# Retention two row tiles ahead of the output projection, and a later, halved split of one weight piece

## The chip, the cores and the metric

The kernel runs on one core of a Trainium2 chip. The metric is the device time of one launch in microseconds (us). Work is done by TensorE (PE), VectorE (DVE), ScalarE (ACT) and GpSimd (POOL); SyncE (SP) issues DMAs. Each engine executes its own list of instructions strictly in order, and an instruction that waits for another engine holds everything behind it on its own engine.

## The reference

Two layers are applied to 512 latent tokens and 128 context tokens of width 1024. Each layer mixes tokens in three groups of heads (A window attention, B neighbourhood attention, C retention), puts the concatenated result through one output projection, and then runs a mixture of 16 experts. The change sits between retention and the output projection:

```python
# group C, per head: chunks of 128 tokens, a state S carried from chunk to chunk, both directions
inner = einsum(einsum(qc, kc) * dmat, vc)
cross = einsum(qc, S) * xi
...
def _retention_out(o, g, gn_w):
    mu = o.mean(-1); var = square(o - mu).mean(-1)          # per token and head
    on = (o - mu) * rsqrt(var + eps) * gn_w
    return silu(g) * on

def _mixer_latent(...):
    oa, ob, oc = window_attention, neighbourhood_attention, retention
    cat = concatenate([oa, ob, _retention_out(oc, gc, gn_w)], -1)   # 512 + 256 + 256 columns
    return cat @ w_out                                              # 1024 x 1024
...
x = layernorm(alpha * x + g1 * mix)
x = layernorm(alpha * x + g2 * expert_choice(x))                    # 16 experts, w_gate_up and w_down
```

## The kernel before

**Tiles.** The 640 tokens are five row tiles of 128: t = 0 to 3 latent, t = 4 context. For each tile `cs` holds the concatenated mixer output, transposed and split into a rounded high half and a remainder. `split` makes the two: ACT writes the high half (L344), DVE or POOL subtracts it for the low half (L345). One product of the output projection is three matmuls, high x high, high x low, low x high (L348, L349, L350 in `mm3`). Columns 0 to 767 of `cs` come from the attentions, columns 768 to 1023 from retention, so the products ko = 6 and 7 of a tile need its retention.

**Output weights.** They come as four pieces of 1 MB, which `weights` loads and splits: pieces 1 and 2 (the upper and lower rows of the first 512 output columns), 3 and 4 (those of the second 512). The names in the rows below are `wh_...` and `wl_...` for the two halves, `w_...` for the raw piece. Piece 1 is split by DVE, piece 2 by POOL (`WO`), piece 3 by DVE, piece 4 by POOL.

**Retention of a tile.** `retention(t, cs)` forms q.k (PE, L1221), multiplies by the decay into the work piece `AT` (DVE, L1225), scales q (DVE, L1230), forms the output `po` (PE, L1239 and L1243), and normalises it: mean (L1247, L1248), subtraction into the work piece `dd` (L1252), square on ACT (L1253), variance (L1255, L1256, L391), inverse root on POOL (L392), and two multiplications (L1259, L1260). Then PE transposes `dd` (L691, two matmuls) and the result is split into `cs`. `AT` and `dd` of all tiles come from one pool named "wr" with two pieces, which alternate, so each `dd` has the same piece as the `dd` of the tile before: L1252 of a tile must wait until L691 of the tile before has read it.

**Order.** NR tiles of retention are made while attention B still runs (`projection`). Then comes a loop over the five tiles: for tile t the first output half is computed (24 matmuls), mixed by `run_all` with the retention of a later tile and with the transposes of z and the router product of tile t - 1 (L1387, ACT L1391, L1395). A second loop computes the second output half of each tile with pieces 3 and 4. `gated` (L1373 to L1375 on DVE) joins an output half to the residual z. A scheduler lays the instructions of each engine into their final order, so the order in the code is only where it starts from; `tc.issue_after(ins)` adds one edge, and only for instructions on the engine of `ins`.

**Slots.** Big tiles share 25 slots of 1 MB, handed out in turn as they come free. `Ahead.fill` issues the loads of the next weights into them, from output weights to expert weights (wgu, wdn).

Of the kernel before, what the change touches and what calls it, by code (L numbers as in the profile page):

```python
# [24 lines left out]
NT = NTOK // 128  # L25
# [49 lines left out]
YS = 1  # L75
PR = "ro"
PGS = "gs"
NR = 1
WG = 1
WO = "0101"  # L80
PZ = "orz"
# [41 lines left out]
AH_P = 1  # L123
KP = 2
# [118 lines left out]
def hybrid_backbone_kernel(ctx: ExitStack, tc: tile.TileContext, a: dict):  # L243
# [41 lines left out]
    V, S, G, T = nc.vector, nc.scalar, nc.gpsimd, nc.tensor  # L285
    queue = [nc.sync]

    def ld(out, in_):
        return queue[0].dma_start(out, in_)
# [3 lines left out]
    def f32(x):  # L293
        return x.bitcast(F32)
# [14 lines left out]
    def weights(n, keep, parts=1, after=None, E=V, s_after=None):  # L309

        if n < 9:
            ahead.fill(n, keep)
            raw = ahead.next()
            hi, lo = sl.get(F32R, "wh"), sl.get(F32R, "wl")
        else:
            hi = sl.get(F32R, "wh")
            ahead.fill(n, keep)
            raw = ahead.next()
            lo = sl.again(ahead.spare, F32R, "wl") if ahead.spare is not None else sl.get(F32R, "wl")
            ahead.spare = raw  # L320
        if s_after is not None:
            for i in range(parts):
                w = 2048 // parts
                s = slice(w * i, w * i + w)
                with tc.issue_after(s_after):
                    S.activation(hi[:, s], raw[:, s], AF.Copy)
                with tc.issue_after(after):
                    E.tensor_tensor(lo[:, s], raw[:, s], f32(hi[:, s]), op=ALU.subtract)  # L328
        elif after is not None:
            with tc.issue_after(after):  # L330
                split(hi, lo, raw, parts, E)
        else:
            split(hi, lo, raw, parts, E)
        if n < 9:
            sl.free(raw)
        return hi, lo
# [3 lines left out]
    def split(hi, lo, src, parts=1, E=V):  # L340
        w = src.shape[-1] // parts
        for i in range(parts):
            s = (Ellipsis, slice(w * i, w * i + w)) if parts > 1 else (Ellipsis,)
            hi_op[:] = [S.activation(hi[s], src[s], AF.Copy)]  # L344
            lo_op[:] = [E.tensor_tensor(lo[s], src[s], f32(hi[s]), op=ALU.subtract)]  # L345
# [403 lines left out]
    def mixer(l, h, A, bg):  # L749
# [401 lines left out]
        def states():  # L1151
# [52 lines left out]
            C.update(S0=S0, Sv=Sv, DT=DT, xi=xi)  # L1204
            yield

        def retention(t, cs):
            qC, vcx, gC, Sv, DT, xi = (C[k] for k in ("qk", "vcx", "g", "Sv", "DT", "xi"))
            kC, vC, cxC = qC[:, 1024:2048], vcx[:, 0:1280], vcx[:, 1280:2048]

            def qk(j, x):
                r, aa = rows(j), j // 2
                if t < 4:
                    return (qC if x == 0 else kC)[r, 512 * aa + 128 * t:512 * aa + 128 * t + 128]
                return cxC[r, 256 * x + 128 * aa:256 * x + 128 * aa + 128]
            AT = work("wr")
            ATv = AT.rearrange("p (a h i) -> p a h i", a=2, h=2)
            pas = [psB(), psB()]
            for aa in range(2):
                for hh in range(2):  # L1220
                    T.matmul(pas[hh][:, 128 * aa:128 * aa + 128], qk(2 * aa + hh, 1), qk(2 * aa + hh, 0),  # L1221
                             start=True, stop=True)
            for hh in range(2):
                pa = pas[hh]
                V.tensor_tensor(ATv[:, :, hh, :], pa[:, 0:256].rearrange("p (a i) -> p a i", a=2),  # L1225
                                DT.rearrange("p (a h) i -> p a h i", a=2)[:, :, hh, :], op=ALU.mult)
            if t < 4:
                o = 1024 + 512 * (t % 2)
                qx = m0[0][:, o:o + 512]
                V.tensor_tensor(qx.rearrange("p (a d i) -> p a d i", a=2, d=2),  # L1230
                                qC[:, 0:1024].rearrange("p (a i) -> p a i", a=2)[:, :, None, 128 * t:128 * t + 128]
                                .to_broadcast([128, 2, 2, 128]), xi, op=ALU.mult)
            yield
            po = psA()
            for aa in range(2):
                if t < 4:
                    for d in range(2):
                        o = 256 * aa + 128 * d
                        T.matmul(po[:, 128 * aa:128 * aa + 128], qx[:, o:o + 128],  # L1239
                                 Sv[:, t, aa, d].rearrange("p h e -> p (h e)"), start=(d == 0), stop=False)  # L1240
                for hh in range(2):
                    o = 128 * aa + 64 * hh
                    T.matmul(po[:, o:o + 64], ATv[:, aa, hh, :], vC[:, 256 * t + o:256 * t + o + 64],  # L1243
                             start=(t == 4), stop=(t == 4 or hh == 1))
            p4 = po[:, 0:256].rearrange("p (h e) -> p h e", h=4)
            mu = sm.tile([128, 4], F32, name="mu", tag="mu")
            V.tensor_reduce(mu, p4, axis=AX.X, op=ALU.add)  # L1247
            V.tensor_scalar(mu, mu, 1.0 / HD, None, op0=ALU.mult)  # L1248
            dd = work("wr")
            d4 = dd[:, 0:256].rearrange("p (h e) -> p h e", h=4)  # L1250
            s4 = dd[:, 256:512].rearrange("p (h e) -> p h e", h=4)
            V.tensor_tensor(d4, p4, mu[:, :, None].to_broadcast([128, 4, 64]), op=ALU.subtract)  # L1252
            S.activation(dd[:, 256:512], dd[:, 0:256], AF.Square)  # L1253
            var = sm.tile([128, 4], F32, name="var", tag="var")
            V.tensor_reduce(var, s4, axis=AX.X, op=ALU.add)  # L1255
            V.tensor_scalar(var, var, 1.0 / HD, None, op0=ALU.mult)  # L1256
            rs = sm.tile([128, 4], F32, name="rs", tag="rs")
            rsqrt(rs, var, 4, "rsv")
            V.tensor_tensor(d4, d4, rs[:, :, None].to_broadcast([128, 4, 64]), op=ALU.mult)  # L1259
            V.tensor_mul(dd[:, 0:256], dd[:, 0:256], gC[:, 256 * t:256 * t + 256])  # L1260
            yield
            split(cs[:, 768:1024], cs[:, 1792:2048], ctx_T(dd, 2))

# [31 lines left out]
        def projection():  # L1295
# [4 lines left out]
            yield from prep()  # L1300
            for t in range(NR):
                css[t] = sl.get(F32R, "cs")
# [42 lines left out]
        zs, bss, started, o_last = [], [], set(), []  # L1345
# [141 lines left out]
        wo = [weights(AH_P, KP, E=G if WO[i] == "1" else V) for i in range(2)]  # L1487
        for t in range(NT):
            ret = iter(())
            for u in range(t + 2):  # L1490
                if u == NT or u < NR or u in started:
                    continue
                started.add(u)
                if u < 4:
                    css[u] = sl.get(F32R, "cs")
                ret = retention(u, css[u])
                if u == t:
                    drain(ret)
                else:
                    next(ret)  # L1500
            cs = css[t]
            z = hf.get(F32, "z")
            ld(z, (a["xtok"] if l == 0 else xres)[128 * t:128 * t + 128])
            if l and RZ:
                if t == 0:
                    gb = sl.get(F32, "ln2")
                    in_row_b(a["ln2g"][l - 1:l], gb[:, 0:1024])
                    in_row_b(a["ln2b"][l - 1:l], gb[:, 1024:2048])
                G.tensor_tensor(z, z, gb[:, 0:1024], op=ALU.mult)
                G.tensor_tensor(z, z, gb[:, 1024:2048], op=ALU.add)  # L1510
                if t == NT - 1:
                    sl.free(gb)
            if t < 4:
                split(cs[:, 0:512], cs[:, 1024:1536], catA[:, 512 * t:512 * t + 512])
                src = catB.rearrange("p (j n) -> p j n", j=2)[:, :, 128 * t:128 * t + 128]
                split(cs[:, 512:768].rearrange("p (j n) -> p j n", j=2),
                      cs[:, 1536:1792].rearrange("p (j n) -> p j n", j=2), src)
            if t == 3:
                sl.free(catA)
                hf.free(catB)  # L1520
            zs.append(z)
            bss.append(m1[0][:, 1664 + 12 * t:1676 + 12 * t].rearrange("p (n x) -> p n x", n=2))
            if t < 4:
                drain(run_all(PZ, o=out_half(t, 0, wo), r=ret, z=first_logits(t - 1) if t else iter(())))
            else:
                drain(ret)
# [7 lines left out]
            G.memset(early[0][:, 1024 * i + 512:1024 * i + 768], 0.0)  # L1534
        for x in early[1]:
            G.memset(x[64:96], 0.0)
        wo += [weights(AH_P, KP, E=G if WO[2 + i] == "1" else V) for i in range(2)]
        g1.append(gates(1))
        for t in range(4):
            if t == IW:  # L1540
# [654 lines left out]
```

## Time and profile before

| | before |
|---|---|
| median of 3 runs | 1911.55 us (1911.55 to 1911.81) |
| profiled execution, its own time | 1910.83 us |
| its span | 1909.1 us, so 1.7 us lie around it |
| busy | PE 95%, DVE 60%, ACT 22%, POOL 13% |
| chain that ended last | PE 56%, DMA 35%, DVE 5% |

The span is what the profile covers; the time is what a run reports. PE works in nearly all of the span, so idle time of PE in the mixing part is what other engines can add or take. The chain goes through DMA in 35% of the span, in the expert part.

### The profile page before, as it was taken

The page shows a single profiled execution, that of the slowest core. Times are in us where ns is not written, and L with a number is a line of the kernel's source. Part 1 is how long each engine was busy: PE and PEld are TensorE (multiplying, and loading weights), DVE is VectorE, ACT ScalarE, POOL GpSimd, SP SyncE. Part 2 cuts the span into 40 slices and gives each one's busy share as a digit, 9 for nine tenths or more (in the row PEclk, how much of TensorE's full clock was granted, in tenths as well). Part 3 has the DMA queues.
Part 4 walks back from the last instruction along what each step waited for, and adds up shares of the span by engine and source line. Part 5 has one row for each costly group of instructions (what it writes and reads, how often), then busy time and mean ns, then how long its engine had stood idle before and what let it go on. Part 6 is the DMA issues. An engine that isn't in the chain of part 4 may idle for free.

```text
span 1909.1 us, 34582 instructions
## 1 busy us (share of the span) xinstructions
PE 1804.8 (95%) x14223; PEld 901.1 (47%) x14223; DVE 1137.1 (60%) x2968; ACT 423.9 (22%) x898; POOL 242.0 (13%) x188
## 2 busy tenths in 40 slices
PE   6999999899999999999879999998899999999995
PEld 3866777773333332222257767787533333222222
DVE  3654537566565655475586555574685757465657
ACT  2354533221000000000153655322200000000002
POOL 3200002221100000000061000121300000000003
PEclk9999999998999999999989999998899999999998
DMA  9333544289999999999933343325999999999994
GB/s 375 117 134 138 200 152 134 108 322 347 397 398 397 397 398 400 401 408 415 400 115 131 127 141 135 107 83 209 345 399 400 399 397 399 398 398 407 408 416 165
DMA packets 95886, 554.62 MB, mean 291 GB/s; under 512 B 13818, under 2 KB 18832, under 8 KB 36336
## 3 DMA queue, kind: packets, MB, share of 16 engines
q1 hardware_dynamic: 89776, 532.71, 70.7%
q0 software_dynamic: 5952, 19.69, 4.3%
q8 instruction: 112, 1.84, 0.4%
q14 instruction: 46, 0.38, 0.1%
HBM read 526.31 MB, written 26.05 MB: 289 GB/s over the span
## 4 chain that ended last, share of the span: by engine, by line
PE 56%; DMA 35%; DVE 5%; issue 2%; ACT 1%; POOL 0%; SPq 0%; DVEq 0%; ACTq 0%; POOLq 0%
DMA w<-wgu 22%; DMA w<-wdn 10%; PE pA L1723 10%; PE pA L348 7%; PE pA L349 6%; PE pA L350 6%; PE pA L1727 5%; PE pB L1723 3%; PE pB L356 2%; PE pC L813 2%; PE pB L1727 2%; PE pA L517 2%; PE pA L917 1%; PE pB L1395 1%; PE pA L1485 1%
## 5 line engine op out<-in xcount | busy, mean ns | idle before, releaser
L1723 PE MATMUL pA<-w,xT 128*32 128x512 f32 x4096 | 488.3, 597 | 12.0 <-DMA w<-wgu 9.3
L1723 PEld LDWEIGHTS pA<-w,xT 128*32 128x32 f32 x4096 | 130.0, 110 | 326.3 <-issue 275.7
L1727 PE MATMUL pA<-w,xT 128*32 128x512 f32 x2048 | 263.8, 592 | 0.0
L1723 PE MATMUL pB<-w,g 128*32 128x512 f32 x1920 | 229.8, 596 | 7.1 <-DMA w<-wdn 7.1
L1727 PEld LDWEIGHTS pA<-w,xT 128*32 128x32 f32 x2048 | 66.2, 110 | 153.6 <-issue 153.0
L1723 PEld LDWEIGHTS pB<-w,g 128*32 128x32 f32 x1920 | 61.2, 110 | 154.9 <-issue 122.4
L1727 PE MATMUL pB<-w,g 128*32 128x512 f32 x960 | 124.8, 592 | 0.0
L1642 DVE STREAM_TRANSPOSE g<-z 32x128 f32<-32x128 f32 x384 | 116.2, 303 | 6.4
L1642 DVE STREAM_TRANSPOSE catB<-xg 32x256 f32<-32x256 f32 x240 | 104.4, 435 | 4.0
L348 PE MATMUL pA<-hhi,wh 128*128 128x512 f32 x224 | 92.0, 411 | 0.0
L350 PE MATMUL pA<-hhi,wl 128*128 128x512 f32 x224 | 88.2, 396 | 0.6 <-DVE wl L328 0.6
L349 PE MATMUL pA<-hlo,wh 128*128 128x512 f32 x224 | 88.2, 394 | 0.0
L1805 POOL DMA_INDIRECT acc<-catB,idx x22 | 31.3, 1424 | 437.6 <-DVE catB L1801 437.6
L1765 ACT ACTIVATE z<-pA 128x512 f32<-128x512 f32 x18 | 10.7, 597 | 336.8 <-DVE xT L1659 165.6
L1642 DVE STREAM_TRANSPOSE g<-xg 32x128 f32<-32x128 f32 x240 | 72.6, 303 | 3.9
L345 DVE TENSOR_TENSOR wl<-w,wh 128x1024 fp32r<-128x1024 f32 (+2 forms) x46 | 54.5, 1220 | 33.4 <-ACT wh L344 13.9
L1623 POOL DMA_INDIRECT xg<-znd,idx x30 | 35.1, 1171 | 293.4 <-DVE catB L1642 238.6
L348 PE MATMUL pA<-wh,cs 128*128 128x512 f32 x160 | 68.0, 426 | 0.5 <-DVE gC L1140 0.3
L344 ACT ACTIVATE wh<-w 128x1024 fp32r<-128x1024 f32 (+2 forms) x50 | 53.7, 1119 | 61.9 <-DMA w<-win 25.0
L1727 PEld LDWEIGHTS pB<-w,g 128*32 128x32 f32 x960 | 31.1, 110 | 72.6 <-issue 72.6
L348 PE MATMUL pA<-wh,hhi 128*128 128x256 f32 x192 | 59.5, 313 | 5.7 <-ACT hhi L344 3.8
L350 PE MATMUL pA<-wh,cs 128*128 128x512 f32 x160 | 64.5, 405 | 0.0
(530 smaller groups left out, 2918.7 us busy)
## 6 DMA issues: line engine op xcount, KB each, us to landing
w<-wgu SPq DMA_DIRECT2D x256, 1024.0 KB, 21.5
w<-wdn SPq DMA_DIRECT2D x128, 1024.0 KB, 21.3
wada<-wada SPq DMA_DIRECT2D x48, 1024.0 KB, 4.9
w<-win SPq DMA_DIRECT2D x20, 1024.0 KB, 7.1
w<-wout SPq DMA_DIRECT2D x8, 1024.0 KB, 5.2
znd<-z SPq DMA_DIRECT2D x8, 512.0 KB, 5.7
acc<-z SPq DMA_DIRECT2D x8, 512.0 KB, 14.8
bias<-bias SPq DMA_DIRECT2D x8, 384.0 KB, 4.8
```

The costliest lines, as they stand in the source:

```text
L344: hi_op[:] = [S.activation(hi[s], src[s], AF.Copy)]
L345: lo_op[:] = [E.tensor_tensor(lo[s], src[s], f32(hi[s]), op=ALU.subtract)]
L348: T.matmul(out, lh, rh, start=first, stop=False)
L349: T.matmul(out, lh, rl, start=False, stop=False)
L350: return T.matmul(out, ll, rh, start=False, stop=last).ins
L356: T.matmul(out, (lh, ll)[x], (rh, rl)[y], start=first, stop=last)
L517: T.matmul(pm[32 * g:32 * g + 32, :], mst[:, k, :], w[:, 512 * g:512 * g + 512], start=(k == 0), stop=(k == 7))
L813: T.transpose(pt[:, 128 * b:128 * b + 128], s[:, o + 128 * b:o + 128 * b + 128], ident)
L1623: r = G.indirect_dma_start(out=xg[0:CAP, 0:1024], out_offset=None, in_=znd[l], in_offset=IndirectOffsetOnAxis(ap=idx[:, e:e + 1], axis=0))
L1642: sq_last[:] = [V.transpose(out, rows.rearrange("p (k q f) -> p k q f", q=4, f=32)[:, :, q, :])]
L1723: last_of["T"] = T.matmul(p[32 * g:32 * g + 32], x[:, 64 * ko + 32 * i:64 * ko + 32 * i + 32], w[:, 512 * n:512 * n + 512], start=(ko == 0 ...
L1727: last_of["T"] = T.matmul(p[32 * g:32 * g + 32], x[:, 512 + 32 * ko:544 + 32 * ko], w, start=first, stop=last).ins
```

## The change

Three things change in both layers. `NR` goes from 1 to 2, so the retention of tile 1 is also made while attention B runs. The loop starts the retention of tile t + 2 beside the first output half of tile t, where it was t + 1. The split of piece 3 becomes two halves of 128x1024 where it was one of 128x2048, and its DVE instructions get an edge behind the last instruction (L1260, now L1262) of the last retention; ACT's part of it has no edge. Lines of the retention stand two further down in the new file.

```diff
-NR = 1
+NR = 2
...
+        r_last = []
+
         def retention(t, cs):
...
-            V.tensor_mul(dd[:, 0:256], dd[:, 0:256], gC[:, 256 * t:256 * t + 256])
+            r_last[:] = [V.tensor_mul(dd[:, 0:256], dd[:, 0:256], gC[:, 256 * t:256 * t + 256]).ins]
...
-            for u in range(t + 2):
-                if u == NT or u < NR or u in started:
+            for u in range(t + 3):
+                if u >= NT or u < NR or u in started:
                     continue
...
-        wo += [weights(AH_P, KP, E=G if WO[2 + i] == "1" else V) for i in range(2)]
+
+        wo.append(weights(AH_P, KP, 2, after=r_last[0]))
+        wo.append(weights(AH_P, KP, E=G))
```

On PE, before, the end of the first output half in layer 0: the retention of tiles 3 and 4 (L1243 reads `vcxC`, the values) and the transposes of tile 3 (L691). Here tile 4's q.k and output products (rows 4 to 9) stand ahead of tile 3's transposes.

```order
L1243 MATMUL pA<-vcxC_1865,work_86 128x64 [waits DVE_49]
L1239 MATMUL pA<-S_102_2672,m_101_2647 128x128 x2
L1243 MATMUL pA<-vcxC_1865,work_86 128x64 x2
L1221 MATMUL pB<-vcxC_1865 128x128 [waits PE_49]
L1221 MATMUL pB<-vcxC_1865 128x128
L1221 MATMUL pB<-vcxC_1865 128x128 [waits DVE_49]
L1221 MATMUL pB<-vcxC_1865 128x128
L1243 MATMUL pA<-vcxC_1865,work_86 128x64 [waits DVE_49] x2
L1243 MATMUL pA<-vcxC_1865,work_86 128x64 x2
L691 MATMUL pC<-cst,work_86 128x128 [waits DVE_49]
```

The transposes of tile 4 stood 24 rows further down, behind twelve matmuls of the second output half (`wh_3288` is piece 3); these are the last rows of those and what follows.

```order
L348 MATMUL pA<-wh_3288,cs_2909 128x512
L349 MATMUL pA<-wl_3289,cs_2909 128x512
L350 MATMUL pA<-wh_3288,cs_2909 128x512
L691 MATMUL pC<-cst,work_86 128x128 [waits DVE_49,PE_49]
L691 MATMUL pC<-cst,work_86 128x128
```

On PE now, the same place: the last output products of tile 4's retention (L1245), the rest of tile 3's first half (`cs_3071`, `wh_2995` is piece 2), the transposes of tile 4, those of z, the router product, and then the second half.

```order
L1245 MATMUL pA<-vcxC_1865,work_86 128x64 x2
L1397 MATMUL pB<-m_106_2894,work_85 128x16 x2
L349 MATMUL pA<-wl_2996,cs_3071 128x512
L350 MATMUL pA<-wh_2995,cs_3071 128x512
L348 MATMUL pA<-wh_2995,cs_3071 128x512
L349 MATMUL pA<-wl_2996,cs_3071 128x512
L350 MATMUL pA<-wh_2995,cs_3071 128x512
L691 MATMUL pC<-cst,work_86 128x128 [waits DVE_49,PE_49]
L691 MATMUL pC<-cst,work_86 128x128
L1389 MATMUL pC<-cst,z_3162 128x128 [waits DMAHW4_49]
L1389 MATMUL pC<-cst,z_3162 128x128 x3
L1397 MATMUL pB<-m_106_2894,work_85 128x16 [waits Activation_49]
```

Tile 4's transposes have moved from behind twelve matmuls of the second half to five matmuls behind the products that they depend on.

On PE now, a little earlier: the transposes of tile 1 (first two rows), the six matmuls of tile 1 that need them (`cs_2947`), and the transposes of tile 2.

```order
L691 MATMUL pC<-cst,work_86 128x128 [waits DVE_49]
L691 MATMUL pC<-cst,work_86 128x128
L348 MATMUL pA<-wh_2995,cs_2947 128x512 [waits Activation_49]
L349 MATMUL pA<-wl_2996,cs_2947 128x512
L350 MATMUL pA<-wh_2995,cs_2947 128x512 [waits DVE_49]
L348 MATMUL pA<-wh_2995,cs_2947 128x512
L349 MATMUL pA<-wl_2996,cs_2947 128x512
L350 MATMUL pA<-wh_2995,cs_2947 128x512
L691 MATMUL pC<-cst,work_86 128x128 [waits DVE_49,PE_49]
L691 MATMUL pC<-cst,work_86 128x128
L1389 MATMUL pC<-cst,z_3009 128x128 [waits DMAHW1_49,PE_49]
```

Between the transposes of tile 2 and of tile 3 there now stand four L1389, six matmuls of tile 2, four L1397 and two L1223. Before, whole output halves lay between the transposes of two tiles.

On DVE, the low half of piece 3, before (third row), ahead of the normalisation of tiles 3 and 4:

```order
L345 TENSOR_TENSOR cs_3033<-pC,cs_3033 128x256 [waits Activation_49]
L1225 TENSOR_TENSOR work_86<-pB,m_101_2647 128x2x128 [waits PE_49]
L345 TENSOR_TENSOR wl_3289<-w_3286,wh_3288 128x2048 [waits DMAHW0_49]
L1402 COPY m_106_2894<-pB 128x16 [waits PE_49]
L1373 TENSOR_TENSOR work_86<-pA,catB_1836 128x512 [waits PE_49]
L1247 TENSOR_REDUCE mu<-pA 128x4 [waits PE_49]
```

Now its two halves stand behind the last multiplication of tile 4's retention:

```order
L1262 TENSOR_TENSOR work_86<-work_86,gC_1866 128x256 [waits DVE_49]
L345 TENSOR_TENSOR wl_3289<-w_3286,wh_3288 128x1024 [waits DMAHW0_49]
L345 TENSOR_TENSOR wl_3289<-w_3286,wh_3288 128x1024
L345 TENSOR_TENSOR cs_419<-pC,cs_419 128x256 [waits Activation_49]
L1404 COPY m_106_2894<-pB 128x16 [waits PE_49]
```

Further up, on SP of layer 0, the load of piece 2 has moved from directly behind that of piece 1 to behind the four stores of `o_st` (L1193) and two loads of z. POOL's split of piece 2, which the load of piece 3 waits for (it goes into piece 2's raw slot), moves with it.

## Rows read from the trace of the kernel before

**Rows 1.** The page's chain that ended last, by engine.

```profile
PE 56%; DMA 35%; DVE 5%; issue 2%; ACT 1%; POOL 0%; SPq 0%; DVEq 0%; ACTq 0%; POOLq 0%
```

**Rows 2.** Waits of PE, 320 to 402 us: total, times, longest.

```profile
PE pC L691 <- DVE work L1260: 3.5, 1, 3.5
PE pC L1387 <- DVE z L1374: 1.6, 1, 1.6
PE pA L1243 <- DVE work L1225: 0.8, 1, 0.8
PE pB L1395 <- ACT work L1391: 0.5, 1, 0.5
```

**Rows 3.** Timeline of PE in layer 1: start, duration, instruction.

```profile
1294.49 0.69 PE L691 MATMUL pC<-cst,work 128*128 128x128 f32 x2 [3.52 <-DVE work L1260]
```

**Rows 4.** Windows, both layers: busy of PE, PEld, DVE, ACT, POOL; PEclk, DMA share, GB/s.

```profile
360.00:370.00 10.00, 5.68 (x34) 4.77 (x33) 6.71 (x20) 1.73 (x4) 1.43 (x2) 0.72 0.81 315
370.00:380.00 10.00, 9.54 (x51) 7.99 (x50) 3.49 (x8) 2.90 (x3) 5.15 (x2) 0.93 0.10 13
...
1290.00:1300.00 10.00, 6.39 (x27) 5.66 (x27) 6.11 (x18) 2.00 (x5) 2.01 (x2) 0.65 0.64 247
1300.00:1310.00 10.00, 9.54 (x43) 7.71 (x44) 2.07 (x5) 2.62 (x3) 4.57 (x1) 0.84 0.24 88
```

**Rows 5.** Timeline of DVE, layer 0, the normalisation of tiles 3 and 4.

```profile
357.26 2.28 DVE L345 TENSOR_TENSOR wl<-w,wh 128x2048 fp32r<-128x2048 f32 x1
...
360.69 0.42 DVE L1247 TENSOR_REDUCE mu<-pA 128x4 f32<-128x256 f32 x1 [0.37 <-PE pA L1243]
...
366.43 0.43 DVE L1260 TENSOR_TENSOR work<-work,gC 128x256 f32<-128x256 f32 x1
367.63 0.42 DVE L1252 TENSOR_TENSOR work<-pA,mu 128x256 f32<-128x256 f32 x1 [0.78 <-PE pC L691]
...
371.66 0.41 DVE L1260 TENSOR_TENSOR work<-work,gC 128x256 f32<-128x256 f32 x1
```

**Rows 6.** Timeline of PE, layer 0.

```profile
353.85 0.96 PE L1395 MATMUL pB<-m,work 128*128 128x16 f32 x8
...
355.37 0.44 PE L691 MATMUL pC<-cst,work 128*128 128x128 f32 x2
355.65 0.60 PE L1387 MATMUL pC<-cst,z 128*128 128x128 f32 x4
356.18 0.71 PE L1221 MATMUL pB<-qkC 64*128 64x128 f32 x4
...
366.91 0.69 PE L691 MATMUL pC<-cst,work 128*128 128x128 f32 x2 [3.52 <-DVE work L1260]
...
372.64 0.40 PE L348 MATMUL pA<-wh,cs 128*128 128x512 f32 x1
372.87 0.39 PE L349 MATMUL pA<-wl,cs 128*128 128x512 f32 x1
```

**Rows 7.** Timeline of ACT, layer 0, split of piece 4 and of tile 4.

```profile
372.15 1.92 ACT L344 ACTIVATE wh<-w 128x2048 fp32r<-128x2048 f32 x1 [3.07 <-DVE work L1260]
375.12 0.38 ACT L344 ACTIVATE cs<-pC 128x256 fp32r<-128x256 f32 x1 [1.04 <-PE pC L691]
375.55 0.60 ACT L1391 ACTIVATE work<-pC 128x512 f32<-128x512 f32 x1
```

**Rows 8.** Timelines of POOL and DVE, layer 0, POOL's split of piece 2.

```profile
325.54 4.58 POOL L345 TENSOR_TENSOR wl<-w,wh 128x2048 fp32r<-128x2048 f32 x1 [0.19 <-ACT wh L344]
...
325.55 4.58 DVE L1982 SCALAR_TENSOR_TENSOR GBT<-modT,lnT 128x2 f32<-128x2 f32 x1
330.06 0.21 DVE L1981 TENSOR_SCALAR GBT<-modT,lnT 128x2 f32<-128x2 f32 x1
```

**Rows 9.** Issues by SP, layer 0, and the page's DMA issues (us to landing).

```profile
319.35 2.69 SPq L1193 DMA_DIRECT2D o_st<-kvs  x4
...
w<-wout SPq DMA_DIRECT2D x8, 1024.0 KB, 5.2
```

## Prediction

> **What bounds the kernel now.** I began with the chain that ended last [rows 1]: PE carries 56% of it, DMA 35%, DVE 5%. The DMA part belongs to the expert weights. The change acts before the experts, where PE is the engine that the end waits for, so I asked the waits of PE over layer 0's output projection next [rows 2]. Four matter, 6.4 us in all: 3.5 us at the transposes of tile 3 (for L1260), 1.6 us at the transposes of z (L1387, for the residual), 0.8 us at tile 4's retention product, and 0.5 us at the router product, for ACT. Layer 1 has the same largest wait [rows 3], and I take its others for equal. Then the windows, for the clock [rows 4]: the granted clock was 0.72 and 0.93 in the two windows around that wait in layer 0, 0.65 and 0.84 in layer 1, a mixture of the levels 2.4 and 1.2 GHz that follows the idle time. The lost shares, 0.35 and 0.51 of 10 us, mean 7.0 and 10.2 us at the low level. At most 3.5 us of each is the idle time itself, so 3.5 to 7.0 and 6.7 to 10.2 us of work ran at half rate. The loss is half of that: 1.8 to 3.5 and 3.4 to 5.1 us, 6.8 us for both layers in the middle.
>
> **Why a tile's retention takes its time.** Two spacings decide. First, from the output product to the transposes of the same tile: L1247 begins at 360.69 as the product ends, L1260 ends at 366.86 [rows 5], so 6.2 us with the other DVE work between. Second, from one tile's transposes to the next tile's. Their pieces of "wr" are the same memory, so L1252 must wait for L691 of the tile before, and the row says so: L691 at 366.91 [rows 6], L1252 of the next tile at 367.63, released by L691, L1260 ended at 372.07 [rows 5]. That is 5.2 us, however early the products were made. Where PE has less than 5.2 us of work between two L691, or less than 6.2 us behind a tile's products, it stands idle for the difference.
>
> **The change part by part.** No matmul is added or removed. What counts is how much work of PE lies between those points in the new order. One 128x512 matmul takes 0.23 us from start to start (372.64 to 372.87), the two L691 0.28 (355.37 to 355.65), the four L1387 0.53 (to 356.18), eight L1395 and four L1221 together 1.52 (353.85 to 355.37) [rows 6].
>
> *Tile 1 to tile 2.* Six matmuls, 1.4 us, and L691 itself: 5.2 - 1.4 - 0.3 = 3.5 us idle. A part of it falls before the six matmuls, which wait for tile 1's split.
>
> *Tile 2 to tile 3.* L691, four L1389, six matmuls, the router product and two L1223: 0.3 + 0.5 + 1.4 + 1.5 = 3.7, so 1.5 us idle.
>
> *Tile 4.* Before, its transposes stood behind twelve matmuls of the second half and no wait is listed for them. Now the second half stands behind them. Between its products and L691 lie five matmuls (1.15) and half of a router product (0.45): 6.2 - 1.6 = 4.6 us idle.
>
> *Router product behind it.* ACT splits the high half of piece 4 only once L1260 has released its slot (at 372.15, just behind 372.07), and only then tile 4's and the transposes of z: 1.92 + 0.38 + 0.60 = 2.9 us [rows 7]. PE has L691 and L1389 meanwhile, 0.8 us. In the old order the rest of the time was covered to 0.5 us; now 2.1 us stay open.
>
> *Sum of these.* 3.5 + 1.5 + 4.6 + 2.1 = 11.7 us idle per layer, where 6.4 stood. The old four waits go: tile 3's 3.5 and tile 4's 0.8, because the products are made a tile earlier; the 1.6 at z, because output matmuls of the next tile now stand in front; and the 0.5 is in the 2.1. Net 5.3 per layer, **10.5 us** for two.
>
> *Piece 3.* Its 2.28 us on DVE [rows 5] stood ahead of the normalisation of tiles 3 and 4; now two halves stand behind all of it. That frees DVE, but the spacings above hold without it. The first half is due 1.2 us behind L1262, and the second half of the projection needs it only after L691, L1389 and the late router product, 2.9 us behind: it costs nothing while that wait is there, and up to 1.2 us if it is not. The ACT part has no edge and waits for its load alone.
>
> *Piece 2's load.* Its place on SP is now behind the stores of o_st, issued at 319.35 and for 2.69 us, and two loads of z. A load of wout takes 5.2 us to land [rows 9], then ACT needs 1.9 us and POOL 4.6, so POOL's split, which ran from 325.54 [rows 8], would end near 336; piece 3 follows late, and ACT has its two halves ahead of tile 0's split. How much of this PE feels, no row shows. Lower bound 0: PE has other tiles' matmuls. Upper bound 4.6 us per layer, one POOL split held against DVE: while POOL's split ran, a DVE operation of two SBUF inputs on 128x2 elements took 4.58 us, where its neighbours take 0.21 [rows 8]. Until now this fell on small vectors for which nobody waited; now the operations of the first retention stand there. I take 1.5 per layer, nearer to the lower end because twelve and more matmuls of attention tiles stand between, **3.0 us** in all.
>
> The Trainium skill has a rule on this (SBUF — State Buffer, "SBUF: two separate sides"): DVE and GpSimd share a port pair as an exclusive lock, and whoever starts first, a GpSimd operation or a DVE operation with two SBUF inputs against a GpSimd one that reads SBUF, blocks the other entirely. The trace agrees with 4.58 beside 0.21 us. By that rule the upper bound would be paid whenever the two meet; by the row it is paid only if PE waits for that DVE work.
>
> *Clock.* Each layer has one idle of 3.5 us before, and has one of about 3.5 and one of 4.6 after. I count the same loss, 0 more, between 6.8 us less (no window at the low level) and 6.8 us more (each layer pays twice).
>
> **Sum.** 10.5 + 3.0 + 0 = 13.5 us. On the profiled execution's 1910.83 us this is 1924.3; the median lies 0.7 above that execution, so **1925 us**. Delay in the projection is passed on in full, I assume: the slots that the expert weights go into come free when PE has used them.
>
> **Rivals.** A. *Faster.* The retention being a tile ahead, its chain is done before PE comes, and PE's order has no waits: the 6.4 us of each layer and the 6.8 of clock go, 19.6 in all, to 1892; half of it to 1902. It decides at the transposes of tiles 2 and 4: they would need 5.2 and 6.2 us of work in front, 22 and 27 matmuls, and have six and five. For it speaks that DVE loses the 2.28 us in front of the chain, and that the six-matmul gap could shrink if L1254 did not wait for L691. Against it is the released-by row of L1252. Chance 0.15.
>
> B. *No change that a measurement can tell.* Idle time moves from tile 3 to tile 4, and what is lost is taken up because the expert stage waits for DMA in a third of the chain [rows 1]: 1911.5, if weight loads start no later than before. Against it: they wait for slots. Chance 0.10.
>
> C. *Slower, by POOL's split.* The upper bound of piece 2's term is paid: 10.5 + 9.2 = 19.7, 1931 us. Speaks for it: the order puts the split beside the retention of tile 0. Chance 0.12.
>
> D. *Slower, by the clock.* The two idles lie some ten us apart, and the clock falls at each: 13.5 + 6.8 = 20.3, 1932 us. Chance 0.13.
>
> **How the numbers follow.** The forecast, slower by 4 to 17 us, has 0.50. A change of 0.2% is 3.8 us, about what a measurement of this kernel can tell from no change. Slower: 0.50 + 0.12 + 0.13 = 0.75; same 0.10; faster 0.15. The forecast's own range: 10.5 with the clock wholly spared and no term for piece 2 is 3.7 us, 1915; with both C and D together 26.5, 1938. A range that holds eight in ten must reach into B and the edge of A: 1907 to 1936. Beyond lie most of A and a little of C with D.
>
> **What will show it.** If I am right, PE's waits in 320 to 402 us list L691 three times (for L1262), the longest 4 to 5 us, and a wait of about 2 at L1397 for ACT; that at L1389 for z is gone; their sum is near 12 where 6.4 stood, in either layer. PEclk stays below 0.9 in two windows per layer or more. If A holds, L691 has no wait over 1 us and PEclk is 1.00. If C holds, PE waits for DVE at L1241 or L1245 or at a tile's split before 345 us. If B holds, the second half starts later but the first expert matmul does not. I would be wrong above all if DVE or ACT were ahead of PE by more than the order tells, since the order has no times: PE might reach these places late for another reason, and then the waits are paid already.

## The result: 0.9% slower, and the profile after

The changed kernel takes 1928.67 us (median of 5 runs, 1923.27 to 1930.47) beside 1911.55 us before: 1.0087 of its time, 95% interval 1.0071 to 1.0103, 17.1 us more. Its profiled execution has a span of 1925.5 us.

The page's chain that ended last, of the changed kernel: PE's part has grown from 56 to 67% [rows 1].

```profile
PE 67%; DMA 25%; DVE 4%; ACT 2%; issue 1%; POOL 0%; SPq 0%; DVEq 0%; ACTq 0%; POOLq 0%
```

PE's waits in layer 0 of the changed kernel, 320 to 410 us (us in total, times, longest), which answer to [rows 2]:

```profile
PE pC L691 <- DVE work L1262: 7.5, 2, 4.7
PE pB L1397 <- ACT work L1393: 1.1, 1, 1.1
PE pA L348 <- DVE work L1375: 0.8, 1, 0.8
PE pA L1241 <- DVE work L1254: 0.5, 1, 0.5
PE pA L348 <- ACT cs L344: 0.5, 1, 0.5
PE pA L1245 <- DVE work L1227: 0.3, 1, 0.3
```

The 3.5 us at tile 3 and the 1.6 us at z are gone; two waits at L691 of other tiles have come, 7.5 us together. Layer 1 lists the same 7.5 and 1.1. The timeline of PE in layer 0 says which tiles they are. The rows of L691 are tiles 1, 2, 3 and 4:

```profile
352.31 0.38 PE L691 MATMUL pC<-cst,work 128*128 128x128 f32 x2
353.17 0.50 PE L348 MATMUL pA<-wh,cs 128*128 128x512 f32 x1 [0.47 <-ACT cs L344]
...
357.68 0.66 PE L691 MATMUL pC<-cst,work 128*128 128x128 f32 x2 [2.86 <-DVE work L1262]
...
364.35 0.69 PE L691 MATMUL pC<-cst,work 128*128 128x128 f32 x2
...
380.86 0.66 PE L691 MATMUL pC<-cst,work 128*128 128x128 f32 x2 [4.67 <-DVE work L1262]
...
383.51 1.89 PE L1397 MATMUL pB<-m,work 128*128 128x16 f32 x8 [1.15 <-ACT work L1393]
```

Tile 2's transposes come 5.37 us after tile 1's. DVE's rows of tile 2 show what lies between: its subtraction (L1254) is released by tile 1's L691, its last multiplication (L1262) ends at 357.53.

```profile
352.73 0.42 DVE L1254 TENSOR_TENSOR work<-pA,mu 128x256 f32<-128x256 f32 x1 [2.80 <-PE pC L691]
...
357.13 0.40 DVE L1262 TENSOR_TENSOR work<-work,gC 128x256 f32<-128x256 f32 x1
```

The windows of layer 0 (busy of PE, PEld, DVE, ACT, POOL; PEclk, DMA share, GB/s) show the second half of the loss:

```profile
350.00:360.00 10.00, 6.66 (x28) 5.09 (x28) 5.67 (x14) 2.12 (x5) 1.01 (x1) 0.84 0.00 0
360.00:370.00 10.00, 10.00 (x35) 8.32 (x34) 4.27 (x10) 0.98 (x2) 1.01 (x1) 0.50 0.13 40
370.00:380.00 10.00, 6.19 (x33) 4.94 (x32) 3.67 (x11) 0.42 (x1) 1.01 (x1) 0.97 0.45 170
380.00:390.00 10.00, 8.00 (x25) 6.64 (x26) 3.54 (x6) 2.67 (x3) 4.59 (x1) 0.54 0.41 157
390.00:400.00 10.00, 10.00 (x51) 8.31 (x50) 2.93 (x9) 2.28 (x3) 0.55 (x1) 0.95 0.41 159
```

PEclk is the granted clock as a share of 2.4 GHz. PE is busy from end to end in 360 to 370 us, and does 35 instructions' work where 390 to 400 us has 51: it runs at 1.2 GHz (0.50), after the idle at tile 2, and again after the idle at tile 4.

Longer windows split the loss. They hold the same stretch of work (the same count of PE's records, in brackets), layer 0's output projection and then layer 1's; first the kernel before:

```profile
320.00:421.00 101.00, 94.35 (x520) 80.04 (x520) 63.07 (x195) 25.93 (x43) 30.67 (x22) 0.97 0.54 196
1245.78:1352.00 106.22, 99.81 (x540) 84.94 (x539) 64.81 (x194) 24.55 (x44) 30.45 (x22) 0.95 0.52 190
```

and the changed kernel:

```profile
320.00:434.40 114.40, 103.61 (x520) 86.92 (x519) 61.16 (x193) 24.52 (x42) 30.68 (x22) 0.90 0.49 182
1257.70:1368.20 110.50, 101.32 (x540) 86.24 (x539) 61.23 (x193) 25.25 (x44) 30.76 (x22) 0.94 0.50 183
```

Layer 0 takes 13.4 us more: idle time (length less busy) rises from 6.65 to 10.79, 4.1 us, and the same 520 instructions are busy 9.3 us longer. Layer 1 takes 4.3 us more: 2.8 idle, 1.5 busy. Together 17.7 us, 6.9 of idle and 10.8 of slower work, where the two profiled executions differ by 16.5 us in all. Most of the delay is passed on. The first expert matmul of layer 0 and transposes behind layer 1's first projection, in the timeline of PE of the kernel before:

```profile
434.64 14.65 PE L1723 MATMUL pA<-w,xT 128*32 128x512 f32 x112 [1.17 <-DVE xT L1696]
...
1228.96 0.38 PE L691 MATMUL pC<-cst,work 128*128 128x128 f32 x2
```

and of the changed kernel, 13.8 and 12.4 us later:

```profile
448.45 14.19 PE L1727 MATMUL pA<-w,xT 128*32 128x512 f32 x112 [1.61 <-DVE xT L1700]
...
1241.38 0.38 PE L691 MATMUL pC<-cst,work 128*128 128x128 f32 x2
```

### The profile page after: what moved, and what is told of

It is laid out like the page before. It is cut to its first block, busy times and chain, and to the rows that moved or that the text cites. A ratio compares the mean times of both kernels' runs of the same rounds, so it can differ in the third digit from the quotient of the medians.

```text
span 1925.5 us, 34577 instructions
## 1 busy us (share of the span) xinstructions
PE 1814.7 (94%) x14223; PEld 911.6 (47%) x14223; DVE 1130.0 (59%) x2970; ACT 423.1 (22%) x900; POOL 242.4 (13%) x188
## 4 chain that ended last, share of the span: by engine, by line
PE 67%; DMA 25%; DVE 4%; ACT 2%; issue 1%; POOL 0%; SPq 0%; DVEq 0%; ACTq 0%; POOLq 0%
DMA w<-wgu 15%; PE pA L1727 14%; DMA w<-wdn 8%; PE pA L348 7%; PE pA L1731 7%; PE pA L349 7%; PE pA L350 7%; PE pB L1727 6%; PE pB L1731 3%; PE pB L356 2%; PE pC L813 2%; PE pA L517 2%; PE pA L917 1%; PE pB L1397 1%; PE pA L1487 1%
## 5 line engine op out<-in xcount | busy, mean ns | idle before, releaser
L350 PE MATMUL pA<-hhi,wl 128*128 128x512 f32 x224 | 88.2, 396 | 0.0
L1769 ACT ACTIVATE z<-pA 128x512 f32<-128x512 f32 x18 | 10.7, 597 | 336.9 <-DVE xT L1663 165.6
L349 PE MATMUL pA<-wl,cs 128*128 128x512 f32 x160 | 66.0, 412 | 0.0
L350 PE MATMUL pA<-wh,cs 128*128 128x512 f32 x160 | 66.0, 412 | 0.0
```

Of the source, the lines that this page charges most:

```text
L349: T.matmul(out, lh, rl, start=False, stop=False)
L350: return T.matmul(out, ll, rh, start=False, stop=last).ins
```

## The experiments

All times are medians beside runs of the kernel before on the same chip (1911.85, 1909.69, 1910.44 and 1911.51 us in the four groups).

**One part at a time.** Three kernels undo parts. First the retention two tiles ahead, with the old split of piece 3:

```diff
-        wo.append(weights(AH_P, KP, 2, after=r_last[0]))
-        wo.append(weights(AH_P, KP, E=G))
+        wo += [weights(AH_P, KP, E=G if WO[2 + i] == "1" else V) for i in range(2)]
```

> Retention two tiles ahead alone; piece 3 split as in the kernel before (one 128x2048 on DVE, no edge). Theory (the place of the transposes in PE's order costs the time, the late split costs nothing): no faster than the changed kernel, 1926 to 1934 us, since the 2.28 us subtraction now stands inside the normalisation of tile 1 and can lengthen the wait at tile 2's transposes from 2.9 towards 5 us; 4.7 at tile 4 stays. Rival (the split behind the retention is what costs): back to 1911 to 1916 us, with the second half no longer waiting.

Measured: 1931.47 us, 1.0095 [1.0070, 1.0119]. The two waits at L691 are the same, and in layer 0 of the traced execution (1933.87 us, the slowest of four) a third has come:

```profile
PE pC L691 <- DVE work L1262: 7.5, 2, 4.7
PE pA L1245 <- DVE work L1227: 3.4, 1, 3.4
```

Tile 2 again follows tile 1 by 5.37 us (358.08, 363.45). The 2.28 us split of piece 3 runs at 349.19, in tile 1's normalisation, where PE has other work: tile 2's wait did not grow, which I had allowed for. So the two waits come without the new split. The third wait is the price of POOL's split of piece 2, rival C's mechanism: POOL's split starts at 333.50 us and takes 4.54, a DVE operation beside it takes 4.50 us, and PE waits for the row behind it.

```profile
334.10 4.50 DVE L1232 TENSOR_TENSOR m<-qkC,m 128x512 f32<-128x512 f32 x1
338.52 0.41 DVE L1227 TENSOR_TENSOR work<-pB,m 128x256 f32<-128x256 f32 x1
338.99 0.69 PE L1245 MATMUL pA<-vcxC,work 128*128 128x64 f32 x2 [3.39 <-DVE work L1227]
```

Second, the new split alone: the kernel before with the two lines that the first took out, and `r_last`.

> The halved split behind the last retention alone; the retention one tile ahead as before. Theory: small loss, 1913 to 1921 us: tile 4's transposes now stand behind one matmul of the second half where twelve stood, so 5.2 us of spacing less about 3.3 us of work leave 1.9 us idle per layer, and the second half waits up to 1 us for the first half of the piece; the 3.5 us at tile 3 stay. Rival (the split is the main cost of the change): 1922 to 1930 us.

Measured: 1920.41 us, 1.0045 [1.0030, 1.0061], at the upper end of the theory. Alone, the split costs half of what the whole change costs, and this does not add up with the first. The mechanism is not the expected one. Tile 4's transposes do stand behind one matmul of the second half now, but no wait is listed for them in the traced execution (1914.31 us, the fastest of six). The new waits of layer 0 are 1.4 us early on, behind a low half of `cs` on DVE that POOL's split of piece 2 holds for 4.39 us (326.87), and 2.0 us at the transposes of z. There POOL's split of piece 4 holds DVE's joining of z for 4.96 us, which takes 0.69 elsewhere, and PE starts as it ends; PEclk is 0.67 and 0.70 in 370 to 390 us.

```profile
373.55 4.61 POOL L345 TENSOR_TENSOR wl<-w,wh 128x2048 fp32r<-128x2048 f32 x1 [3.56 <-ACT wh L344]
373.76 4.96 DVE L1376 SCALAR_TENSOR_TENSOR z<-z,work 128x512 f32<-128x512 f32 x1
378.82 0.85 PE L1389 MATMUL pC<-cst,z 128*128 128x128 f32 x4 [1.96 <-issue]
```

In the whole change the last two do not meet (POOL's split of piece 4 starts at 382.78 us there), so this wait is not a part of the 17 us. What the slower runs of this kernel add to the traced one is not shown.

Third, `NR = 2` alone, with the loop and the split of before:

```diff
-            for u in range(t + 3):
+            for u in range(t + 2):
```

> NR = 2 alone: tile 1's retention is also made beside attention B, but the loop stays one tile ahead (t + 2) and the split of piece 3 is the old one. Theory: PE's order at the end of the first half is the old one, so the time is that of the kernel before, 1908 to 1914 us, with 3.5 us at tile 3's transposes. Rival (the earlier retention of tile 1, with the late piece 2 and POOL's split beside it, costs by itself): 1917 us or more.

Measured: 1910.08 us, 0.9995 [0.9984, 1.0006]: no change, with one wait of 3.3 us at tile 3's transposes, as before. The first and the third run differ in that one line alone. So the lead in the loop costs the time, and the earlier retention of tile 1 costs nothing that can be measured. Nor does the late piece 2 by itself cost a time that can be measured: POOL's split of it starts at 332.01 us here too and holds a DVE operation for 3.88 us, and PE waits 1.0 us behind it.

**The clock.** The changed kernel with matmuls of a constant in the idle time:

```diff
+FILL = {2: 7, 4: 10}
...
+            p = psC()
+            if t in FILL:
+                with tc.issue_after(tr_last[0] if t < 4 else po_last[0]):
+                    for _ in range(FILL[t]):
+                        T.matmul(p[:, 256:512], ident, cst[:, 0:256], start=True, stop=True)
```

(`tr_last` is the last L691, `po_last` the tile's last output product.)

> The changed kernel with matmuls of a constant (128x256, results not used) in the idle time: 7 behind tile 1's transposes and 10 behind tile 4's retention products, 0.44 us each by the 44 records in 9.66 us at the end of the projection, so 7.5 us per layer of added PE work. Theory (about half of the loss is the low clock behind the idle): PE stays at the high level, no wait over 1.5 us at the transposes, 1912 to 1920 us although work is added. Rival (the clock costs nothing of note, the idle is all): no gain, 1926 to 1932 us.

Measured: 1912.62 us, 1.0006 [0.9993, 1.0020], 16 us less than the changed kernel although each layer does 7.5 us more work. No wait at the transposes of any tile is left (they are line 1274 of that kernel), and the clock stays at the high level:

```profile
360.00:370.00 10.00, 9.96 (x52) 7.93 (x51) 6.85 (x19) 1.47 (x4) 1.31 (x1) 1.00 0.45 139
370.00:380.00 10.00, 9.57 (x56) 8.15 (x55) 7.97 (x12) 2.89 (x3) 5.66 (x2) 1.00 0.45 177
380.00:390.00 10.00, 10.00 (x54) 8.45 (x53) 3.37 (x10) 2.32 (x3) 0.55 (x1) 1.00 0.59 215
```

The added work, 15 us in both layers, is about the idle that it replaces (of 20.0 us in the long windows, 15.1 lie at L691), so most of the gain must come from the clock: the 10.8 us above and the 6.6 us that the kernel before lost already (half of 4.4 and 8.7 us at the low level, below). The fill also moves rows of PE (24 matmuls of 128x512 stand between the transposes of tiles 2 and 3, where there were six), so that it is the clock's alone is not shown.

**The shared piece.** The normalised values of even and odd tiles in two halves, the squares in the tile's decay piece:

```diff
-            dd = work("wr")
-            d4 = dd[:, 0:256].rearrange("p (h e) -> p h e", h=4)
-            s4 = dd[:, 256:512].rearrange("p (h e) -> p h e", h=4)
+            o = 256 * (t % 2)
+            dd = work("wr")[:, o:o + 256]
+            sq = AT[:, 0:256]
+            d4 = dd.rearrange("p (h e) -> p h e", h=4)
+            s4 = sq.rearrange("p (h e) -> p h e", h=4)
```

> The changed kernel with the shared piece taken apart: the normalised values of even and odd tiles lie in two halves of the piece, and the squares go into the decay piece of the same tile, so that a tile's subtraction no longer waits for the transposes of the tile before. Theory (the spacing of 5.2 us from transposes to transposes comes from that piece): the subtraction of tile 2 starts before tile 1's transposes, the 2.9 us at tile 2 is gone; at tile 4 some 3 us stay (6.2 us of chain against some 3.1 us of work in front), with one fall of the clock per layer: 1912 to 1921 us. Rival (the chain is slow because DVE is full, the piece is innocent): the wait at tile 2 stays over 2 us or moves whole to tile 3, 1924 to 1931 us.

Measured: 1916.20 us, 1.0033 [1.0023, 1.0043], and the wait at tile 2 is gone, 3.1 us at tile 4 are left:

```profile
345.01 0.44 PE L691 MATMUL pC<-cst,work 128*128 128x128 f32 x2
352.65 0.39 PE L691 MATMUL pC<-cst,work 128*128 128x128 f32 x2
362.61 0.39 PE L691 MATMUL pC<-cst,work 128*128 128x128 f32 x2
369.04 0.41 PE L691 MATMUL pC<-cst,work 128*128 128x128 f32 x2 [3.10 <-DVE work L1264]
```

One expectation failed: tile 2's subtraction still starts behind tile 1's transposes (346.44 after 345.01). The wait went because the scheduler, free of that edge, put 24 matmuls between the two, not because the chain got shorter. Some 10 of the 17 us hang on that edge, by way of the order; what the chain takes when nothing is shared, this run does not show.

**Less fill, and versions that might win.** Five and four constant matmuls where there were seven and ten:

> The changed kernel with fewer constant matmuls in the idle time, 5 behind tile 1's transposes and 4 behind tile 4's products, 4.0 us per layer where the run with 17 had 7.5. Theory (the fill costs its own time once the clock stays up): 7 us less than that run, 1903 to 1909 us, with PEclk 1.00 in all windows. Rival (the fill must cover the idle whole): idle of over 2 us and a low clock come back, 1914 us or more.

Measured: 1928.37 us, 1.0094 [1.0065, 1.0122]; the theory missed by 20 us. The waits at the tiles' transposes are gone here too, but another has come, in both layers. One row each of POOL, DVE and PE:

```profile
377.35 4.59 POOL L346 TENSOR_TENSOR wl<-w,wh 128x2048 fp32r<-128x2048 f32 x1 [3.78 <-ACT wh L345]
377.46 5.03 DVE L1387 SCALAR_TENSOR_TENSOR z<-z,work 128x512 f32<-128x512 f32 x1
382.60 0.63 PE L1400 MATMUL pC<-cst,z 128*128 128x128 f32 x4 [3.33 <-issue]
```

POOL's split of piece 4 starts 0.1 us ahead of DVE's joining of z, which takes 5.03 us where its neighbour of the same form takes 0.69. PE stands 3.3 us at the transposes of z (the row names no releaser, but they start 0.1 us after DVE's row ends, at 382.49), and the clock falls (0.66 in 380 to 390 us). The same kernel with piece 4 split by DVE:

```diff
-        wo.append(weights(AH_P, KP, E=G))
+        wo.append(weights(AH_P, KP, E=V))
```

> The run with 9 constant matmuls again, but piece 4 split by DVE where POOL did it. There POOL's split of piece 4 began at 377.3 us and DVE's joining of z (two SBUF inputs) took 5.03 us instead of 0.69, PE stood 3.3 us at the transposes of z, and the clock fell. Theory (POOL's split holds DVE there): no DVE operation of that kind over 1 us, no wait over 2 us at the transposes of z, clock up, 1903 to 1910 us. Rival (too little fill): the idle of over 2 us and the low clock stay, 1920 us or more.

Measured: 1915.89 us, 1.0022 [1.0011, 1.0033]. From 366 to 394 us DVE has no operation over 1 us but the splits, the longest wait at z is 1.6 us, PEclk is 1.00 from 350 to 400 us: the mechanism is as stated, and 12.5 us lie between the two medians. The size is not: its ten runs lie at 1910 to 1911 and at 1915 to 1918 us, none at 1903 to 1910, and the one execution with a trace is of the lower group. Why the 7 us of saved fill don't show stays open.

Both, the piece taken apart and four constant matmuls behind tile 4's products:

> Both: the piece taken apart, and only 4 constant matmuls (1.8 us per layer) behind tile 4's products. Theory (spacing, then clock): no wait over 1.5 us at any transposes, clock up throughout, 1897 to 1906 us, faster than the kernel before. Rival (the new wait of the decay piece for the squares takes the gain back): waits for DVE at the output products (L1248) of 2 us or more, 1908 us or more.

Measured: 1905.34 us, 0.9975 [0.9964, 0.9987]: faster than both kernels, by a quarter of a per cent over the one before. Waits for DVE of 2.7 us (layer 0, at L1244) and 1.6 us (layer 1) are there, but not by the rival's mechanism. In layer 0 PE waits for a subtraction (L1260) behind a DVE operation that POOL's split of piece 2 held:

```profile
332.66 4.51 POOL L346 TENSOR_TENSOR wl<-w,wh 128x2048 fp32r<-128x2048 f32 x1 [1.52 <-ACT wh L345]
334.38 3.34 DVE L1235 TENSOR_TENSOR m<-qkC,m 128x512 f32<-128x512 f32 x1 [2.33 <-PE pA L1244]
338.86 0.86 PE L1244 MATMUL pA<-S,m 128*128 128x128 f32 x4 [2.65 <-DVE work L1260]
```

In layer 1 the held row is L1254, 3.76 us. PEclk is 1.00 from 350 to 400 us, but 0.87 in 340 to 350, behind the 2.7 us. No run gives piece 2 to DVE; what that would be worth stays open. The same with the old split of piece 3:

> Two tiles ahead with the piece taken apart and 4 constant matmuls as in the fastest run, but piece 3 split as in the kernel before, so that tile 4's transposes can stand behind twelve matmuls of the second half. Theory: no wait at tile 2 and tile 4; tile 3's transposes follow tile 3's products by some 3.7 us of work where the chain takes 6.2, so 2.5 us of idle per layer there, with a low clock in one of the layers perhaps: 1904 to 1913 us. Rival (order with the late split is better for another reason): 1915 us or more.

Measured: 1913.83 us, 1.0015 [1.0006, 1.0025], just above the theory, and the wait is at another tile than expected: 1.9 us at tile 2's transposes, where the old split of piece 3 (2.29 us on DVE) stands ahead of that tile's normalisation, and none at tile 3's. Behind it the clock falls in 350 to 370 us (0.82, 0.83). With six matmuls of fill for four:

> The fastest run so far with 6 constant matmuls where it had 4, 0.9 us per layer more work. Eight of its ten runs lay at 1904 to 1906 us with a mean granted clock of 0.981 to 0.983, two at 1910 to 1911 with 0.978. Theory (in those two the clock fell behind a rest of idle): the two are gone and the median is 1905 to 1908 us. Rival (the fill only adds its time): 1906 to 1909 us, with slower runs as often as before.

Measured: 1910.41 us, 0.9998 [0.9986, 1.0011]. Neither: the median is higher than either theory or rival allowed, and its runs spread from 1905.83 to 1917.2. Inconclusive; in the one trace, of the fastest run, POOL's split of piece 4 holds DVE's joining of z again, for 4.05 us, and PE waits 0.9 us behind it. And the fastest run with piece 4 split by DVE:

> The fastest run so far, with piece 4 split by DVE where POOL did it. In that run no DVE operation was held by POOL's split of piece 4 (none but the split of piece 3 over 0.9 us from 366 to 394 us). Theory: nothing to gain there, 1903 to 1908 us. Rival (2.3 us more on DVE in front of tile 4's split and of z delay the second half): 1909 us or more.

Measured: 1904.75 us, 0.9964 [0.9953, 0.9974], the lowest median, though its interval overlaps that of the same kernel with POOL's split (0.9964 to 0.9987), so a gain by DVE's split is not shown. In layer 0, up to 425 us, three waits of PE are left, and the 1.6 us at z, which was in the kernel before, is not among them:

```profile
PE pC L1402 <- issue: 2.8, 1, 2.8
PE pA L1244 <- DVE work L1260: 1.9, 1, 1.9
PE pB L1410 <- ACT work L1406: 0.2, 1, 0.2
```

**Before, with a fill.** Eight constant matmuls behind tile 3's products in the kernel before (`FILL = {3: 8}`):

> The kernel before with 8 constant matmuls (3.5 us per layer) behind tile 3's output products. In its order tile 3's transposes then stand behind eleven matmuls of the second half, and tile 4's behind six matmuls from there. Theory: the 3.5 us at tile 3 go, but tile 4's transposes must now keep 5.2 us from tile 3's with 1.9 us of work between, so some 3 us of idle come back there and the added work is paid: 1909 to 1918 us. Rival (tile 3's wait and its low clock were all): 1900 to 1906 us.

Measured: 1921.43 us, 1.0055 [1.0039, 1.0072], slower than expected by 3 us. The mechanism is the expected one: tile 3's wait is gone, tile 4's transposes stand 5.38 us behind tile 3's, with the wait there, and the clock falls:

```profile
368.17 0.38 PE L1272 MATMUL pC<-cst,work 128*128 128x128 f32 x2
373.55 0.41 PE L1272 MATMUL pC<-cst,work 128*128 128x128 f32 x2 [2.86 <-DVE work L1264]
```

After tiles 1 and 2 of the changed kernel and of the first run, that is a third kernel and another pair of tiles with 5.4 us between transposes that have little work between them (L1272 here). In the run with 17 constant matmuls tile 2 follows tile 1 by 5.07 us without a wait, so the chain needs no more than that there.

## Why the prediction was right

*Direction and size.* 1925 us forecast, 1928.67 measured. The forecast mechanism is there: slower because tile 2's and tile 4's transposes stand too close behind what they depend on. The sum came out by two errors that cancel in part, idle time of 6.9 us where 13.5 were forecast and slower work of 10.8 us where none was, so that the size came so near is in part luck. Of the signs, two waits at L691 are listed and not three, PE's listed waits add up to 10.7 and 9.1 us where 12 were expected, and PEclk is below 0.9 in three windows of ten us in each layer.

*The spacings.* 5.2 us from transposes to transposes was 5.37; 6.2 us of chain behind tile 4's products gave 4.6 us of idle and was 4.67. Tile 2: 3.5 forecast, 2.86 and 0.47 measured. These rested on the released-by row of L1252 [rows 5], and the new L1254 has the same releaser. That the shared piece alone makes the distance is argued from these rows; the run without it changed the order too.

*Terms that were too high.* Tile 3's 1.5 us is not there, and the router product waits 1.15 where I had 2.1: PE ran at the low level at both places, so the same work covered more time (tile 2's L691 to tile 3's took 6.67 us in layer 0, 5.45 in layer 1). Idle rose by 6.9 us in both layers together, where the sum had 13.5 with piece 2's term in it.

*Piece 2.* 1.5 us per layer assumed. POOL's split ended at 336.73 us, where the forecast had 336, and held DVE as feared, but PE felt little of it: 0.3 us at L1245 in layer 0, for the L1227 right behind the held row, and nothing in layer 1. The 0.5 us for L1254 and the 0.8 us for L1375 are of another kind: this L1254 starts when tile 0's L691 releases it, and L1375 when PE's own L350 does. DVE's and POOL's rows of the changed kernel:

```profile
332.93 4.34 DVE L1232 TENSOR_TENSOR m<-qkC,m 128x512 f32<-128x512 f32 x1
...
332.16 4.57 POOL L345 TENSOR_TENSOR wl<-w,wh 128x2048 fp32r<-128x2048 f32 x1 [3.25 <-ACT wh L344]
```

The Trainium skill's exclusive lock (SBUF — State Buffer, "SBUF: two separate sides") agrees with this row, with 5.03 us in the run with less fill, and with its end when DVE did that split. Whether PE waits is read from the rows behind: 0.3 us here, 3.3 us there.

*The clock, the step that was mis-sized.* "I count the same loss, 0 more", between 6.8 less and 6.8 more. The busy time for the same work rose by 9.3 us in layer 0 and 1.5 in layer 1, 10.8 in all, beyond the bound. I had priced one fall by its length in the kernel before; after the 2.86 us at tile 2 the low level lasted from 357.7 to some 370.5 us (the last long matmul starts at 370.13), 12.8 us, where after the 3.5 us of the kernel before it lasted from 366.9 to some 371.3, 4.4 us. Layer 1 shows that the length is not fixed: there, the same wait at tile 2 (2.87 us, until 1294.72) is followed by the low level from 1295.5 to some 1299.0 us, 3.5 us, and by PEclk 1.00 to 1310 us (these ends are read in windows of 0.5 us). The window that holds it all:

```profile
1295.00:1300.00 5.00, 4.96 (x24) 4.12 (x22) 3.40 (x10) 1.28 (x3) 1.01 (x1) 0.66 0.00 0
```

The second fall, at tile 4, cost work at the low level in both layers: 8.9 and 7.9 us. In layer 1 the kernel before had a longer low stretch already, 8.7 us from 1294.5 to 1303.2. So the work at the low level rose from 4.4 to 21.7 us in layer 0 and from 8.7 to 11.4 in layer 1; half of the rise is 10.0 us, about the 10.8. Rival D, the clock falling at both places, is what happened beside the forecast idle, dear in layer 0 and cheap in layer 1.

*The rivals.* A fell at the two places that it named: the chains of tiles 2 and 4 were not done when PE came (those of tiles 1 and 3 were). B fell: of 13.8 us at the start of layer 0's experts 12.4 were still there behind layer 1's first projection, so the loads took up 1.4 at most. C's hold of DVE is there, its price is not in this kernel: 0.3 us. Two of its neighbours paid it, 3.4 us with the old split of piece 3 and 2.7 and 1.6 us in the first kernel that was faster than the one before.

## What to carry to other kernels

A producer that is started earlier helps only if the consumer's place in the in-order list leaves it the chain's length of other work; read the distance between the two in the new order, in work and not in rows, against the chain's length in the old trace. Where neighbours share a buffer, look for a smallest distance between their consumers (5.1 to 5.4 us here): a head start of a tile did not shorten it. When a list is rescheduled for one edge, look where the other waits went and which engines now meet: the split's edge alone cost 0.45%, by a hold of DVE that was not expected, and the lead and the edge together cost no more than the lead.

## What the runs showed that was not expected

An idle of 2.9 us on PE was followed by 12.8 us at 1.2 GHz in one layer and by 3.5 us in the other, so what it cost beyond its own length varies from 1.7 to 6.4 us. Constant matmuls that took as long as the idle at L691 gave back 16 us. And POOL's split of a 128x2048 piece held a DVE operation of 0.69 us for 5.03 us when it started 0.1 us ahead of it, while in the changed kernel no such operation fell beside the same split of piece 4 (4.59 us from 382.78), no wait of PE follows from it, and a DVE operation with one input in PSUM (`pC`) took its usual 0.42 us beside it. An operation with a single SBUF input can be held too: in layer 1 of the changed kernel L1250 (`mu<-mu`, 0.16 us elsewhere) took 3.21 us, until POOL's split of piece 2 ended.
